# Opening of a two-layer hybrid trunk: first norm, modulation and first projection in an order fixed by hand

## The chip, the cores and the metric

One core of a Trainium2 chip runs the whole program. The metric is the time of one execution in device microseconds, taken over several runs; one further execution was recorded by the hardware profiler, and its trace is what the rows below come from. Engines are named as the profile names them: PE (TensorE, matmul), DVE (VectorE), ACT (ScalarE), POOL (GpSimd), SP (SyncE, which here only issues transfers).

## The reference, cut to what matters

The kernel computes two layers over 256 context tokens and 1024 latent tokens, 1280 in all, of width 1024. What the change touches is the first lines of the first layer:

```python
def rmsnorm(x):
    xf = x.astype(jnp.float32)
    return (xf * lax.rsqrt(jnp.mean(xf * xf, axis=-1, keepdims=True) + RMS_EPS)).astype(x.dtype)

def modulate(x, shift, scale):
    return rmsnorm(x) * (1.0 + scale) + shift

for layer in range(DEPTH):
    mod_l = (jax.nn.silu(c) @ w_ada[layer] + b_ada[layer])[:, None, :]
    mod_c = (jax.nn.silu(c_ctx) @ w_ada[layer] + b_ada[layer])[None, None, :]
    sh1_l, sc1_l, g1_l, sh2_l, sc2_l, g2_l = jnp.split(mod_l, 6, axis=-1)
    sh1_c, sc1_c, g1_c, sh2_c, sc2_c, g2_c = jnp.split(mod_c, 6, axis=-1)
    pl = split_proj(modulate(xl, sh1_l, sc1_l) @ w_in[layer])
    pc = split_proj(modulate(xc, sh1_c, sc1_c) @ w_in[layer])
    ...
```

Behind them come four chunkwise scans in both directions (the mixers), an output projection, a squared-ReLU MLP, and the same again for layer two.

## The kernel before

Activations lie feature-major: x is eight tiles of 128 features by 1280 tokens, and `k` counts these tiles. Tokens go in three blocks, `TBS`: 0 to 256 (context), 256 to 768 and 768 to 1280. Every float32 product is made of three matmuls, from a high part and a low part of each operand: `Hhi`, `Hlo` are the parts of the normalised input.

The opening has four pieces of work. First the modulation: `ada_unit` loads 32 pieces of `w_ada` (256 KB each, L382) on SP's queue into 16 slots and multiplies each by the silu of the two conditions (L383, four column groups of the array at a time); `ada_finish` copies, transposes and adds the bias (L389 to L400). Then the norm: `rstd` squares each tile on ACT (L447), adds the squares over features on PE (L448), spreads the sum (L451 ACT, L452 PE), and takes the logarithm and the exponential on ACT (L454, L455). Then `norm_apply`, tile by tile: DVE scales (L477), ACT adds the shift and rounds to `Hhi` (L480), DVE makes `Hlo` (L482). Last the first projection, `denseVS`: its weights `w_vs` (8 tiles, L590) are split on ACT and DVE (L591, L592), and for each of ten chunks of 128 tokens 24 matmuls of 128x304 run over k in one PSUM bank (L601), followed by two evacuations (L604, L605). Next in the program are the transposes of `turn` (L616), the dense products of the other heads (L294 to L296, weights split at L282 and L283), the features of the GLA heads (L787 on PE, L307 on ACT, L313 on DVE) and the scans.

Nothing here has a hand-fixed order: a scheduler sees the whole program and sets the order of every engine's instructions, so products and splits of different pieces interleave. That holds for the scans too: between two steps of a scan (L831, L956, L1000, L1019 on PE) it sets dense matmuls (L294 to L296, L632 to L634) and, on DVE, the next modulation rows (L414).

`params2` and `cond_rows`, some 35 small DVE operations and a store of the conditions to memory that POOL issues (L333), run early, while PE and DVE wait for `w_ada`.

Of the kernel before, what the change touches and what calls it, by code (L numbers as in the profile page):

```python
# [34 lines left out]
def R(ap):  # L35
    return ap.bitcast(F32R)


def F(ap):
    return ap.bitcast(F32)  # L40


class Ring:
# [154 lines left out]
class K:  # L198
# [176 lines left out]
        nc.scalar.activation(self.o["rtd"](24), lg, AF.Exp, scale=128.0)  # L375


    def ada_unit(self, l, r, k, bank, bufs):
        nc = self.nc
        for g in range(4):  # L380
            w = bufs.next()(512)
            nc.sync.dma_start(w, self.io["w_ada"][l, r, k, :, g, :])  # L382
            nc.tensor.matmul(self.bank(bank)[32 * g:32 * g + 32, :], lhsT=self.cc[:, k, :], rhs=w,  # L383
                             start=(k == 0), stop=(k == NK - 1), tile_position=(0, 32 * g))

    def ada_finish(self, l, r, bank, bank2, tmp):
        nc = self.nc
        s = tmp(512)
        nc.scalar.activation(s, self.bank(bank), AF.Copy)  # L389
        T = self.bank(bank2).rearrange("p (c q) -> p c q", q=128)  # L390
        for cb in range(4):
            nc.tensor.transpose(T[:, cb, :], s[:, cb * 128:(cb + 1) * 128], self.ident)
        Tv = self.bank(bank2).rearrange("p (c g j) -> p g c j", g=4, j=32)[:, :, :, 0:2]
        mo = self.mod[:, l, 16 * r:16 * r + 16, :].rearrange("p (g c) j -> p g c j", c=4)
        bb = self.bada[:, l, 16 * r:16 * r + 16].rearrange("p (g c) -> p g c", c=4)
        nc.vector.tensor_tensor(mo, Tv, bb.unsqueeze(3).to_broadcast([128, 4, 4, 2]), op=ALU.add)
        if r in (0, 2):
            a = 8 if r == 0 else 32
            m = self.mod[:, l, a:a + 8, :]
# [26 lines left out]
    def rstd(self, tb, fast=False):  # L426
# [31 lines left out]
    def norm_mod(self, l, tbs, sh, sc):  # L458

        rs = [self.rstd(tbs[0], FAST[0])]  # L460
        for i, tb in enumerate(tbs):
            if i + 1 < len(tbs):
                rs.append(self.rstd(tbs[i + 1], FAST[0]))
            self.norm_apply(l, tb, rs[i], sh, sc)
            yield
# [114 lines left out]
    def denseVS(self, S, sp):  # L580

        nc, t = self.nc, self.nc.tensor
        V = self.get(S, "V")(NC, 256)
        P = self.get(sp, "raw")(NC, 48)
        src = self.io["w_vs"][self.l]

        def load(k):
            raw = self.raw.next()(512)[:, 0:304]
            hi, lo = (R(self.wall.sub(608 * k + 304 * e, 304)(304)) for e in range(2))
            nc.sync.dma_start(raw, src[k])  # L590
            nc.scalar.activation(hi, raw, AF.Copy)  # L591
            nc.vector.tensor_tensor(lo, raw, F(hi), op=ALU.subtract)  # L592
            return hi, lo

        def body(w):
            for c in range(NC):
                ps = self.bank(self.dbanks.next())
                for k in range(NK):
                    h, u = self.hm(k, 128 * c, 128), w[k]
                    for i, (a, b) in enumerate(((0, 0), (0, 1), (1, 0))):  # L600
                        t.matmul(ps[:, 0:304], lhsT=h[a], rhs=u[b], start=(k + i == 0), stop=(k == NK - 1 and i == 2))  # L601
                    if k == 3:
                        yield 1500
                nc.scalar.activation(V[:, c, :], ps[:, 0:256], AF.Copy)  # L604
                nc.vector.tensor_copy(P[:, c, :], ps[:, 256:304])  # L605
                yield 1500
        return Dense(load, NK, body)

    def turn(self, sp):

# [777 lines left out]
    def mix_open(self, l):  # L1388

        self.otbs = TBS if l == 0 else TBS[1:]  # L1390
        pw, (self.wall,) = self.pool(f"pw{l}", [1024 * 5])
        self.wring = Ring([self.wall.sub(1024 * i, 1024) for i in range(5)])
        nx = NK * NT
        left = (self.rest - nx - 5 * 1024) // 8 * 8
        ph, hs = self.pool(f"ph{l}", [left])
        hp = self.heap = Heap(hs)
        self.dbanks = Ring((0, 1, 2))
        self.mb = Ring((4, 5, 6, 7))
        self.mpair = Ring((4, 6))
        self.obank = Ring((3,))  # L1400
        self.sp, self.gl = {}, {}
        vs = self.denseVS(self.gl, self.sp)
        vs.pre(NK)
# [6 lines left out]
        if l == 1:  # L1410
            self.norm_block(l, TBS[-1], 0, 8, fast=FAST[3])
        for (t0, n), _ in zip(TBS, blocks):
            for _ in range(n // 64):
                next(gen, None)
        next(gen, None)
# [157 lines left out]
def build(ctx, tc, io):  # L1573
    b = K(ctx, tc, io)
    b.setup()
    nc = b.nc
    b.l = 0
    b.openX()
    for k in range(NK):
        nc.scalar.dma_start(b.X[k][:, 0:CTX], io["xT"][:, k, 0:CTX])  # L1580
    b.params(b.tmps.next())

    ps, ss = b.pool("ps", [512] * 16)
    bk = b.banks.next()
    ring = Ring(ss)
    for k in range(NK):
        b.ada_unit(0, 0, k, bk, ring)
    b.ada_finish(0, 0, bk, b.banks.next(), b.tmps.next())
    ps.release()
    b.params2(b.tmps.next())  # L1590
    b.cond_rows(b.tmps.next())
    for l in range(2):
        b.l = l
        tbs = TBS if l == 0 else TBS[1:]
# [12 lines left out]
        aring = Ring(zip(cs[nw + nf::2], cs[nw + nf + 1::2]))  # L1607
# [4 lines left out]
        gen = ada1(cs[nw:nw + nf] + tmps.items[4:])  # L1612
# [68 lines left out]
def host(x, c, ctx, c_ctx, w_ada, b_ada, w_in, g_heads, hgrn_lb_logits, ml_gate_bias, rt_decay_logit,  # L1681
         gla_w_a, gla_b_a, w_out, w_ff1, w_ff2, g_final):
    A = {}
    ca = np.ascontiguousarray
# [23 lines left out]
    for d in range(2):  # L1708
        ga[:, 16 * d:16 * d + 16, d, :] = gla_w_a[:, d]
    A["gla_w"] = ga  # L1710
    A["w_ada"] = ca(w_ada[:1, :, :2048].reshape(1, 8, 128, 1, 4, 512).transpose(0, 3, 1, 2, 4, 5))
# [9 lines left out]
    vs = [seg(n) for n in ("gl_v", "gl_a_fwd", "gl_a_bwd")] + [iff[:, :, :, q, :].reshape(2, 1024, 8) for q in range(2)]  # L1721
# [20 lines left out]
```

## Time and profile before

| | us |
|---|---|
| median of 3 runs (lowest, highest) | 3277.83 (3273.87, 3279.31) |
| profiled execution | 3277.57 |
| its span in the trace | 3275.8 |
| PE busy in the span | 3188.0 |
| DVE busy in the span | 2098.3 |
| last matmul of the first projection ends | 90.15 from the span's start |

The profiled execution's time is that of the span and 1.8 us around it. Times in the rows are microseconds from the span's start.

### The profile page before, as it was taken

To read this page: it belongs to the slowest core of one execution; us is meant where nothing else is said; L and a number is where in the kernel's file an instruction comes from. 1 tells how busy PE (TensorE), PEld (TensorE's weight loads), DVE (VectorE), ACT (ScalarE), POOL (GpSimd) and SP (SyncE) were. 2 spreads that over 40 slices of the span, in tenths; PEclk is the share of its full clock that TensorE was granted. 3 is DMA by queue.
4 is the path that set the end of the run, shared out by engine and by line. 5 is a ranking of instruction groups with operands and counts; after the bars stand their busy time and mean duration, and the time that the engine had idled before them with its cause. 6 is when DMAs were issued, how large, how long until landed. Compare 5 with 4: busy or idle time off the path is not lost.

```text
span 3275.8 us, 52563 instructions
## 1 busy us (share of the span) xinstructions
PE 3188.0 (97%) x20681; PEld 2607.3 (80%) x20681; DVE 2098.3 (64%) x4333; ACT 1285.0 (39%) x2665; POOL 11.5 (0%) x42
## 2 busy tenths in 40 slices
PE   7999999999999999999999999999999999999998
PEld 4787788878888888888888677788778888888887
DVE  4778887776588845454545586876756555555546
ACT  4666564545332121212122575764444322222222
POOL 0000000000000000000000000000000000000000
PEclk9999899999999999999999999999999999999999
DMA  6115566345157511111111212333224111111111
GB/s 208 58 61 176 183 186 190 120 134 179 63 165 230 161 39 39 39 39 39 39 39 40 78 64 73 120 109 113 90 72 151 58 46 52 46 52 46 52 49 65
DMA packets 181953, 308.20 MB, mean 94 GB/s; under 512 B 21880, under 2 KB 51240, under 8 KB 181448
## 3 DMA queue, kind: packets, MB, share of 16 engines
q1 hardware_dynamic: 180376, 303.02, 28.8%
q8 instruction: 162, 2.65, 0.3%
q10 hardware_dynamic: 1296, 1.81, 0.2%
q14 instruction: 87, 0.71, 0.1%
q0 software_dynamic: 32, 0.01, 0.0%
HBM read 259.11 MB, written 45.65 MB: 93 GB/s over the span
## 4 chain that ended last, share of the span: by engine, by line
PE 81%; DVE 8%; DMA 6%; ACT 3%; issue 1%; SPq 0%; DVEq 0%; ACTq 0%
PE psum L294 22%; PE psum L295 21%; PE psum L296 21%; PE psum L831 2%; PE psum L601 2%; PE psum L834 1%; PE psum L818 1%; PE psum L632 1%; DMA ph<-w_adaR 1%; PE psum L634 1%; PE psum L633 1%; PE psum L1359 1%; PE psum L706 1%; PE psum L1019 1%; DMA ps<-w_ada 1%
## 5 line engine op out<-in xcount | busy, mean ns | idle before, releaser
L526 DVE SCALAR_TENSOR_TENSOR x<-psum,st,x 128x512 f32<-128x512 f32 (+1 forms) x648 | 440.7, 689 | 203.5 <-PE psum L296 202.8
L282 ACT ACTIVATE pc<-st 128x512 fp32r<-128x512 f32 x256 | 161.2, 632 | 854.4 <-PE psum L295 840.9
L295 PE MATMUL psum<-pc,pc 128*128 128x512 f32 (+1 forms) x1296 | 477.0, 368 | 6.0 <-DVE pc L506 6.0
L294 PE MATMUL psum<-pc,pc 128*128 128x512 f32 (+1 forms) x1296 | 476.1, 367 | 0.0
L296 PE MATMUL psum<-pc,pc 128*128 128x512 f32 (+1 forms) x1296 | 474.7, 366 | 0.0
L294 PE MATMUL psum<-Hhi,pc 128*128 128x512 f32 (+1 forms) x1280 | 471.1, 368 | 1.5 <-ACT pc L282 1.5
L295 PE MATMUL psum<-Hlo,pc 128*128 128x512 f32 (+1 forms) x1280 | 472.0, 369 | 0.1
L296 PE MATMUL psum<-Hhi,pc 128*128 128x512 f32 (+1 forms) x1280 | 470.5, 368 | 0.0
L294 PE MATMUL psum<-Hhi,pw 128*128 128x512 f32 (+1 forms) x1192 | 451.5, 379 | 7.6 <-ACT pw L282 3.5
L295 PE MATMUL psum<-Hlo,pw 128*128 128x512 f32 (+1 forms) x1192 | 447.5, 375 | 0.0
L296 PE MATMUL psum<-Hhi,pw 128*128 128x512 f32 (+1 forms) x1192 | 446.6, 375 | 0.6 <-DVE pw L283 0.6
L505 DVE TENSOR_TENSOR st<-st 128x256 f32<-128x256 f32 (+1 forms) x160 | 101.8, 637 | 301.5 <-ACT pc L504 300.8
L295 PEld LDWEIGHTS psum<-pc,pc 128*128 128x128 f32 x1296 | 245.0, 189 | 48.4 <-DVE pc L506 6.9
L294 PEld LDWEIGHTS psum<-pc,pc 128*128 128x128 f32 x1296 | 245.0, 189 | 44.1 <-DVE x L526 1.2
L296 PEld LDWEIGHTS psum<-pc,pc 128*128 128x128 f32 x1296 | 244.6, 189 | 42.9 <-issue 2.7
L294 PEld LDWEIGHTS psum<-Hhi,pc 128*128 128x128 f32 x1280 | 241.3, 189 | 43.3 <-ACT pc L282 2.4
L295 PEld LDWEIGHTS psum<-Hlo,pc 128*128 128x128 f32 x1280 | 241.3, 189 | 41.0 <-issue 0.5
L283 DVE TENSOR_TENSOR pc<-st,pc 128x512 fp32r<-128x512 f32 x256 | 175.6, 689 | 153.4 <-ACT pc L282 133.5
L296 PEld LDWEIGHTS psum<-Hhi,pc 128*128 128x128 f32 x1280 | 241.1, 188 | 41.0 <-DVE pc L283 0.6
L294 PEld LDWEIGHTS psum<-Hhi,pw 128*128 128x128 f32 x1192 | 227.3, 191 | 53.7 <-issue 9.2
L296 PEld LDWEIGHTS psum<-Hhi,pw 128*128 128x128 f32 x1192 | 227.1, 191 | 39.3 <-issue 2.4
L295 PEld LDWEIGHTS psum<-Hlo,pw 128*128 128x128 f32 x1192 | 227.6, 191 | 37.7 <-issue 2.9
(401 smaller groups left out, 4859.4 us busy)
## 6 DMA issues: line engine op xcount, KB each, us to landing
st<-w_ff SPq DMA_DIRECT2D x256, 256.0 KB
ph<-w_adaR SPq DMA_DIRECT2D x128, 256.0 KB
st<-w_inT SPq DMA_DIRECT2D x96, 256.0 KB
st<-w_adaR SPq DMA_DIRECT2D x74, 256.0 KB
pc<-w_adaR SPq DMA_DIRECT2D x54, 256.0 KB
st<-w_out SPq DMA_DIRECT2D x50, 256.0 KB
d_z<-st SPq DMA_DIRECT2D x40, 256.0 KB
ps<-w_ada SPq DMA_DIRECT2D x32, 256.0 KB
```

The costliest lines, as they stand in the source:

```text
L282: nc.scalar.activation(hi, raw, AF.Copy)
L283: (eng or nc.vector).tensor_tensor(lo, raw, F(hi), op=ALU.subtract)
L294: t.matmul(out, lhsT=w[0], rhs=m[0], start=first, stop=False)
L295: t.matmul(out, lhsT=w[0], rhs=m[1], start=False, stop=False)
L296: t.matmul(out, lhsT=w[1], rhs=m[0], start=False, stop=last)
L505: nc.vector.tensor_tensor(r, r, r, op=ALU.mult)
L526: nc.vector.scalar_tensor_tensor(x, ps, self.mod[:, l, 40 + o, j:j + 1], x, op0=ALU.mult, op1=ALU.add)
L601: t.matmul(ps[:, 0:304], lhsT=h[a], rhs=u[b], start=(k + i == 0), stop=(k == NK - 1 and i == 2))
L632: t.matmul(ps[:, e, :], lhsT=h[0], rhs=u[0], start=(k == 0), stop=False)
L633: t.matmul(ps[:, e, :], lhsT=h[0], rhs=u[1], start=False, stop=False)
L634: t.matmul(ps[:, e, :], lhsT=h[1], rhs=u[0], start=False, stop=(k == NK - 1))
L831: nc.tensor.matmul(o, lhsT=ST[r0:r0 + kd, c, d, :], rhs=qd[d](c)[r0:r0 + kd, :], start=(j == 0), stop=False, tile_position=(r0, 0))
```

## The change

All of the opening of layer 0 moves into one function, `open_first`, whose order holds as written (`manual_schedule`). Every load is on SP's queue. The first 768 tokens of x come first, in eight pieces of 384 KB; a two-element store that reads the fifth of them follows, and behind it come the weights. `w_ada` is laid out anew on the host, as four sets of eight pieces; set q holds what the tiles 2q and 2q+1 need, for shift and scale. The modulation of a set is 32 products of 128 columns (`products`, L402) instead of 8 of 512, so that 128 products replace 32 and the columns stay the same, then one transpose, two additions and one more (`shifts`, L411 to L418). The first two blocks of tokens go two tiles at a time: `apply` for a tile, then `part` for six chunks (c = 0 to 5, six PSUM banks at once), with the products of the next set between the two tiles' parts. The third block's squares, norm, `apply` and its four chunks come behind all of that, tile by tile. `params2` and `cond_rows` stand behind the opening now. Squares were added on PE before, too; the function that does it is written anew.

```diff
+    def open_first(self, vs):
+        aring = Ring([hp.alloc(512) for _ in range(10)])
...
+        def products(ws):
+            for k in range(NK):
+                for g in range(4):
+                    nc.tensor.matmul(self.bank(6)[32 * g:32 * g + 32, 0:128], lhsT=self.cc[:, k, :], rhs=ws[k][:, g, :],
+                                     start=(k == 0), stop=(k == NK - 1), tile_position=(0, 32 * g))
+            s = self.tmps.items[6](128)
+            nc.scalar.activation(s, self.bank(6)[:, 0:128], AF.Copy)
+            return s
...
+        sqs = Ring(self.tmps.items[5:8])
+        def squares(tb, bank):
+            t0, n = tb
+            acc = self.bank(bank)[:, 0:n]
+            for k in range(NK):
+                g = k % 4
+                sq = sqs.next()(n)
+                nc.scalar.activation(sq, self.X[k][:, t0:t0 + n], AF.Square)
+                nc.tensor.matmul(acc[32 * g:32 * g + 32, :], lhsT=self.ones32, rhs=sq, start=(k < 4), stop=(k >= 4),
+                                 tile_position=(0, 32 * g))
...
+        def apply(k, tbs):
+            todo = []
+            for tb in tbs:
...
+                nc.vector.scalar_tensor_tensor(t, self.X[k][:, t0:t0 + n], self.mod[:, 0, 8 + k, j:j + 1], rs[tb],
+                                               op0=ALU.mult, op1=ALU.mult)
+                nc.scalar.activation(R(hi), t, AF.Identity, bias=b)
+                todo.append((lo, t, b, hi))
+            for lo, t, b, hi in todo:
+                nc.vector.scalar_tensor_tensor(R(lo), t, b, hi, op0=ALU.add, op1=ALU.subtract)
+
+        one, two_ = TBS[:2], TBS[2]
+        with self.tc.manual_schedule():
+            self.params(self.tmps.items[3])
+            load_x(0, two)
+
+            nc.sync.dma_start(self.d_e[0, 0, 0:1, 0:2], self.X[4][0:1, 0:2])
+            ws = load_w(0)
+            vs.load_raw(0)
+            vs.load_raw(1)
+            s0 = squares(TBS[0], 0)
+            rms(TBS[0], 1, s0)
+            s1 = squares(TBS[1], 2)
+            s = products(ws)
+            rms(TBS[1], 3, s1)
+            shifts(0, s)
+            vs.split()
+            vs.split()
+            ws = load_w(1)
+            apply(0, one)
+            apply(1, one)
+            for q in range(4):
+                k = 2 * q
+                for c in range(6):
+                    vs.part(c, k, c)
+                if q < 3:
+                    vs.load_raw(k + 2)
+                    vs.load_raw(k + 3)
+                    s = products(ws)
+                    if q < 2:
+                        ws = load_w(q + 2)
+                    else:
+                        load_x(two, NT)
+                for c in range(6):
+                    if c == 3 and q < 3:
+                        shifts(q + 1, s)
+                        vs.split()
+                        vs.split()
+                    vs.part(c, k + 1, c)
+                if q < 3:
+                    apply(k + 2, one)
+                    apply(k + 3, one)
+            s = squares(two_, 6)
+            rms(two_, 7, s)
+            apply(0, (two_,))
+            apply(1, (two_,))
+            for c in range(6):
+                vs.evac(c, c)
+            last = (6, 0, 1, 7)
+            for k in range(NK):
+                if k + 2 < NK:
+                    apply(k + 2, (two_,))
+                for c in range(6, NC):
+                    vs.part(c, k, last[c - 6])
...
         if l == 0:
-            for t0, n in TBS[1:]:
-                for k in range(NK):
-                    self.nc.sync.dma_start(self.X[k][:, t0:t0 + n], self.io["xT"][:, k, t0:t0 + n])
-        gen = iter(vs)
-        blocks = self.norm_mod(l, TBS, 0, 8) if l == 0 else iter(TBS)
...
+            self.open_first(vs)
...
+        if l == 0:
+            self.params2(self.tmps.next())
+            self.cond_rows(self.tmps.next())
...
-    for k in range(NK):
-        b.ada_unit(0, 0, k, bk, ring)
```

Three places in the order show what moves. The first is SP, from the start of the program: the parameters and then `w_ada` stood at the head of its queue before (the pieces of x for the context were on ACT's queue).

```order
L250 DMA st_77<-params 128x416
L382 DMA ps_0_110<-w_ada 128x512
L382 DMA ps_1_111<-w_ada 128x512
L382 DMA ps_2_112<-w_ada 128x512
L382 DMA ps_3_113<-w_ada 128x512
```

Now it begins thus (`ph0_0_100` holds the ten slots of `w_ada`, `d_e_70` is the target of the small store):

```order
L389 DMA x0_4_89<-xT 128x768
L389 DMA x0_5_90<-xT 128x768
L389 DMA x0_6_91<-xT 128x768
L389 DMA x0_7_92<-xT 128x768
L466 DMA d_e_70<-x0_4_89 1x2
L395 DMA ph0_0_100<-w_ada 128x512 x8
L699 DMA st_77<-w_vs 128x304 x2
L395 DMA ph0_0_100<-w_ada 128x512 x8
```

The eight pieces of x and the store have moved ahead of the first weight piece, and each set of `w_ada` is followed by the two tiles of `w_vs` for the same pair.

The second place is DVE at the third block of tokens, the last of the first projection. Before, with the scaling at L477 and `Hlo` at L482 (`st_77` is a temporary, `Hhi_80` what ACT wrote; the first L482 here is still that of the second block's last tile):

```order
L477 SCALAR_TENSOR_TENSOR st_77<-x0_0_85,st_77 128x512
L482 SCALAR_TENSOR_TENSOR Hlo_81<-st_77,Hhi_80 128x512
L477 SCALAR_TENSOR_TENSOR st_77<-x0_1_86,st_77 128x512
L482 SCALAR_TENSOR_TENSOR Hlo_81<-st_77,Hhi_80 128x512
L605 COPY ph0_0_256<-psum_63 128x48 x2
L482 SCALAR_TENSOR_TENSOR Hlo_81<-st_77,Hhi_80 128x512
L477 SCALAR_TENSOR_TENSOR st_77<-x0_2_87,st_77 128x512
L605 COPY ph0_0_256<-psum_63 128x48
L477 SCALAR_TENSOR_TENSOR st_77<-x0_3_88,st_77 128x512
L482 SCALAR_TENSOR_TENSOR Hlo_81<-st_77,Hhi_80 128x512
```

Now, with the scaling at L454, `Hlo` at L459, a weight split at L283 and small operations of `params2` at L340 and behind:

```order
L454 SCALAR_TENSOR_TENSOR st_77<-x0_4_89,st_77 128x512
L459 SCALAR_TENSOR_TENSOR Hlo_81<-st_77,Hhi_80 128x512
L454 SCALAR_TENSOR_TENSOR st_77<-x0_5_90,st_77 128x512
L340 TENSOR_TENSOR st_77<-st_77 128x4
L283 TENSOR_TENSOR pw0_0_96<-st_77,pw0_0_96 128x512
L341 TENSOR_TENSOR st_77<-st_77 128x4
L342 TENSOR_TENSOR st_77<-st_77 128x4
L364 TENSOR_SCALAR st_77<-st_77 128x24
L459 SCALAR_TENSOR_TENSOR Hlo_81<-st_77,Hhi_80 128x512
L454 SCALAR_TENSOR_TENSOR st_77<-x0_6_91,st_77 128x512
```

Scaling and `Hlo` of one tile stand behind each other, so that the scaling of the next tile is queued behind an `Hlo` that waits for ACT; before, the scaling of x0_1 stood ahead of the `Hlo` of x0_0, and that of x0_3 ahead of the `Hlo` of x0_2.

The third place is PE in the last latent scan of layer 0, at the step that follows L831 (in the change L959 is L831, L962 is L834, L1147 is L1019 and L834 is L706). Before:

```order
L1000 MATMUL psum_63<-px0_0_693 64x64 x5
L632 MATMUL psum_63<-pw0_0_252,Hhi_80 128x256
L633 MATMUL psum_63<-pw0_0_252,Hhi_80 128x256
L634 MATMUL psum_63<-pw0_0_252,Hlo_81 128x256
L632 MATMUL psum_63<-pw0_0_252,Hhi_80 128x256
L633 MATMUL psum_63<-pw0_0_252,Hhi_80 128x256
L634 MATMUL psum_63<-pw0_0_252,Hlo_81 128x256
L831 MATMUL psum_63<-px0_0_693,ph0_0_256 128x128 x2
L632 MATMUL psum_63<-pw0_0_252,Hhi_80 128x256
```

Now:

```order
L959 MATMUL psum_63<-ph0_0_100 128x128 x2
L962 MATMUL psum_63<-px0_0_727 64x128 x2
L1147 MATMUL psum_63<-px0_0_727 32x2x32 x8
L1147 MATMUL psum_63<-ph0_0_100,st_77 32x2x32 x7
L834 MATMUL psum_63<-st_77 128x512
L1147 MATMUL psum_63<-ph0_0_100,st_77 32x2x32
L959 MATMUL psum_63<-px0_0_727,ph0_0_100 128x128 x2
L296 MATMUL psum_63<-Hhi_80,pw0_0_96 128x512
```

Dense matmuls that stood between scan rows here stand further behind now. Counted over the order: ahead of the first latent L956 there are 24 more 512-column matmuls of L294 to L296 than before and 24 more of 256 columns; ahead of the last one there are 57 fewer of 512 columns and 230 fewer of L632 to L634 (3 fewer of 256 columns of L294 to L296). On DVE, 51 of the 512-column rows of L414 stand between the first and the last latent L952, where 76 stood, and 15 of L283 where 20 stood. From the layer's output projection on, the two orders are the same.

## Rows read from the trace of the kernel before

**Rows 1.** The page, its span and busy time by engine.

```profile
span 3275.8 us, 52563 instructions
PE 3188.0 (97%) x20681; PEld 2607.3 (80%) x20681; DVE 2098.3 (64%) x4333; ACT 1285.0 (39%) x2665; POOL 11.5 (0%) x42
```

**Rows 2.** Busy time by stage: window, length, engines, PEclk, DMA share, GB/s.

```profile
10.00:20.00 10.00, 5.58 (x24) 1.27 (x24) 5.67 (x40) 3.64 (x15) 0.00 (x0) 1.00 0.99 302
20.00:30.00 10.00, 9.19 (x46) 2.58 (x47) 0.28 (x1) 2.72 (x7) 0.64 (x1) 1.00 1.01 369
```

**Rows 3.** The chain that ended last, 0 to 100: start, length, piece.

```profile
2.11 6.54 DMA ps<-w_ada
...
31.60 3.61 DMA x<-xT
...
37.03 0.48 DVE st L477
37.50 0.39 DVE pw L592
...
64.09 26.06 PE psum L601 x182
```

**Rows 4.** Timeline of PE in the opening: start, length, instruction, count.

```profile
14.42 4.52 PE L383 MATMUL psum<-ps,st 128*32 128x512 f32 x22
...
35.36 0.66 PE L392 MATMUL psum<-st 128*128 128x128 f32 x4 [0.69 <-ACT st L389]
...
38.24 0.41 PE L601 MATMUL psum<-pw,Hhi 128*128 128x304 f32 x1
38.62 1.04 PE L448 MATMUL psum<-st 128*32 128x512 f32 x2
...
42.61 0.83 PE L601 MATMUL psum<-pw,Hhi 128*128 128x304 f32 x4 [1.21 <-ACT Hhi L480]
```

**Rows 5.** Timeline of ACT in the opening.

```profile
24.83 1.54 ACT L447 ACTIVATE st<-x 128x256 f32<-128x256 f32 x4 [6.20 <-PE psum L448]
...
28.75 0.42 ACT L455 ACTIVATE st<-st 128x256 f32<-128x256 f32 x1
...
37.54 0.51 ACT L480 ACTIVATE Hhi<-st 128x256 fp32r<-128x256 f32 x1 [0.33 <-DVE st L477]
...
54.98 0.63 ACT L455 ACTIVATE st<-st 128x512 f32<-128x512 f32 x1
55.76 2.41 ACT L447 ACTIVATE st<-x 128x512 f32<-128x512 f32 x4
...
66.91 0.72 ACT L480 ACTIVATE Hhi<-st 128x512 fp32r<-128x512 f32 x1
```

**Rows 6.** Timeline of DVE at the end of the second block.

```profile
66.13 0.75 DVE L477 SCALAR_TENSOR_TENSOR st<-x,st 128x512 f32<-128x512 f32 x1
66.79 0.75 DVE L482 SCALAR_TENSOR_TENSOR Hlo<-st,Hhi 128x512 fp32r<-128x512 f32 x1
```

**Rows 7.** Timeline of PE in the mixers: dense and narrow matmuls.

```profile
134.88 1.14 PE L818 MATMUL psum<-ph,px 128*32 128x64 f32 x64
331.57 0.40 PE L295 MATMUL psum<-Hlo,pw 128*128 128x512 f32 x1
331.80 0.39 PE L296 MATMUL psum<-Hhi,pw 128*128 128x512 f32 x1
```

**Rows 8.** Busy time by stage in the mixers, columns as in rows 2.

```profile
300.00:345.00 45.00, 34.78 (x326) 26.69 (x325) 41.06 (x100) 27.31 (x56) 0.00 (x0) 0.86 0.40 126
334.00:560.00 226.00, 214.11 (x2031) 177.88 (x2032) 182.40 (x483) 124.19 (x279) 1.29 (x12) 0.96 0.58 184
335.00:353.00 18.00, 12.68 (x64) 8.77 (x63) 12.90 (x28) 8.03 (x16) 0.00 (x0) 0.53 0.27 88
```

**Rows 9.** Timeline of DVE: the first row of the GLA features.

```profile
92.78 0.48 DVE L313 TENSOR_SCALAR px<-psum,st 128x256 f32<-128x256 f32 x1 [0.15 <-ACT st L307]
```

**Rows 10.** DMA issues between 24 and 34: the store of `cond_rows`, size, us to landing.

```profile
d_c<-st POOLq DMA_DIRECT2D x1, 8.0 KB, 4.9
```

More of the change, by code (lines that the diff above doesn't have):

```diff
@@ L375, in params2 @@
         nc.scalar.activation(self.o["rtd"](24), lg, AF.Exp, scale=128.0)
[L378 to L399, printed above, removed]
-            nc.vector.tensor_scalar(m, m, 1.0, None, op0=ALU.add)
@@ new lines, in open_first, with load_x, load_w, shifts @@
+    def open_first(self, vs):
+        nc, io, hp = self.nc, self.io, self.heap
+        aring = Ring([hp.alloc(512) for _ in range(10)])
+        two = CTX + 512
+        rs = {}
+        tn = Ring(self.tmps.items[:4])
+        rbuf = [self.tR.items[0], self.tR.items[1], self.tR.items[0]]
+        def load_x(a, b):
+            for k in range(NK):
+                nc.sync.dma_start(self.X[k][:, a:b], io["xT"][:, k, a:b])
+        def load_w(q):
+            out = []
+            for k in range(NK):
+                w = aring.next()(4, 128)
+                nc.sync.dma_start(w, io["w_ada"][q, k])
+                out.append(w)
+            return out
+        def products(ws):
[6 more added lines that the diff above has]
+            return s
+        def shifts(q, s):
+            T = self.bank(7)[:, 0:128]
+            nc.tensor.transpose(T, s, self.ident)
+            T = T.rearrange("p (g j) -> p g j", j=32)
+            for e in range(2):
+                o = 8 * e + 2 * q
+                bb = self.bada[:, 0, o:o + 2].unsqueeze(2).to_broadcast([128, 2, 2])
+                nc.vector.tensor_tensor(self.mod[:, 0, o:o + 2, :], T[:, 2 * e:2 * e + 2, 0:2], bb, op=ALU.add)
+            m = self.mod[:, 0, 8 + 2 * q:10 + 2 * q, :]
+            nc.vector.tensor_scalar(m, m, 1.0, None, op0=ALU.add)
+        sqs = Ring(self.tmps.items[5:8])
+        def squares(tb, bank):
+            t0, n = tb
+            acc = self.bank(bank)[:, 0:n]
+            for k in range(NK):
+                g = k % 4
[3 more added lines that the diff above has]
+                                 tile_position=(0, 32 * g))
+            s = sqs.next()(n)
+            nc.scalar.activation(s, acc, AF.Copy)
+            return s
+        def rms(tb, bank, s):
+            t0, n = tb
+            bro = self.bank(bank)[:, 0:n]
+            nc.tensor.matmul(bro, lhsT=self.sel, rhs=s, start=True, stop=True)
+            r = rbuf.pop(0)(n)
+            nc.scalar.activation(r, bro, AF.Ln, bias=self.eps)
+            nc.scalar.activation(r, r, AF.Exp, scale=-0.5)
+            rs[tb] = r
+        def apply(k, tbs):
+            todo = []
+            for tb in tbs:
+                t0, n = tb
+                j = 0 if t0 < CTX else 1
+                t = tn.next()(n)
+                b = self.mod[:, 0, k, j:j + 1]
+                hi, lo = self.Hhi[:, k, t0:t0 + n], self.Hlo[:, k, t0:t0 + n]
+                nc.vector.scalar_tensor_tensor(t, self.X[k][:, t0:t0 + n], self.mod[:, 0, 8 + k, j:j + 1], rs[tb],
[51 more added lines that the diff above has]
+            last = (6, 0, 1, 7)
+            for k in range(NK):
+                if k + 2 < NK:
+                    apply(k + 2, (two_,))
+                for c in range(6, NC):
+                    vs.part(c, k, last[c - 6])
+            for c in range(6, NC):
+                vs.evac(c, last[c - 6])
+        hp.free(*aring.items)
+        self.banks = Ring(range(8))
@@ L1402, in mix_open @@
         vs = self.denseVS(self.gl, self.sp)
-        vs.pre(NK)
         if l == 0:
-            for t0, n in TBS[1:]:
-                for k in range(NK):
-                    self.nc.sync.dma_start(self.X[k][:, t0:t0 + n], self.io["xT"][:, k, t0:t0 + n])
-        gen = iter(vs)
-        blocks = self.norm_mod(l, TBS, 0, 8) if l == 0 else iter(TBS)
-        if l == 1:
+            self.open_first(vs)
+        else:
+            vs.pre(NK)
+            gen = iter(vs)
             self.norm_block(l, TBS[-1], 0, 8, fast=FAST[3])
[L1412 to L1415, printed above, removed]
+            for _ in gen:
+                pass
         self.poolX.release()
@@ L1578, in build @@
     b.openX()
-    for k in range(NK):
[L1580 to L1586, printed above, removed]
-        b.ada_unit(0, 0, k, bk, ring)
[L1588 to L1591, printed above, removed]
     for l in range(2):
@@ L1710, in host @@
     A["gla_w"] = ga
-    A["w_ada"] = ca(w_ada[:1, :, :2048].reshape(1, 8, 128, 1, 4, 512).transpose(0, 3, 1, 2, 4, 5))
+    A["w_ada"] = ca(w_ada[0, :, :2048].reshape(8, 128, 2, 4, 256).transpose(3, 0, 1, 2, 4).reshape(4, 8, 128, 4, 128))
     A["w_adaR"] = ca(w_ada.transpose(0, 2, 1).reshape(2, 3, 16, 128, 1024))
```

42 lines of the change are left out of this document (25 added, 17 removed).

## Prediction

> **What bounds the kernel now.** I read the page first: PE is busy for 3188.0 of 3275.8 us [rows 1], so a change of the opening can be worth only what PE stands idle there, or what later work it starts sooner. So the stages come next: 10 to 20 us PE is half idle while the queues move 302 GB/s, and 20 to 30 they move 369 [rows 2]. The chain of waits says the same: up to 31.6 it runs over pieces of `w_ada`, then over x (31.60), and from 64.09 over 182 matmuls of the first projection, 26.06 us long [rows 3]; 26.06/182 gives 0.143 a matmul, and 240 of them are 34.3 us. So x comes too late, since it is queued behind 8 MB of `w_ada`, and the projection starts at 38.24 and runs steadily only from 42.61 [rows 4]. Its last matmul ends at 90.15 (64.09 + 26.06).
>
> **The change, as a sum in us from the span's start.** It is made against the profiled execution, 3277.57, a quarter of a us under the median of 3277.83. What a measurement can tell from no change is about 0.2%, 6.5 us.
>
> A. *x first.* 3.15 MB of x and 0.97 MB of parameters and constants at 345 GB/s, my choice between 302 and 369 [rows 2], from 2.0 (the first piece began at 2.11 [rows 3]): landed at 13.9 (13.2 to 15.6).
>
> B. *Context norm.* The last square takes 0.4 (four take 1.54), and from the end of those squares (26.37) to the end of the exponential (28.75 + 0.42) it took 2.8 [rows 5]: 17.1.
>
> C. *Squares of the second block.* Eight at 2.41/4 = 0.60 on ACT [rows 5]: 21.9; the last addition on PE 1.04 [rows 4]: 23.0. PE has its queue in order, so the products wait behind.
>
> D. *Products of set 0.* The trace has no such matmul. L383's first 22, of 512 columns, took 0.205 each [rows 4]; if that is the lower clock, 128 columns at the upper one take 0.026, and 32 of them 0.8. If none overlap, L392's 0.66/4 = 0.165 [rows 4] gives 5.3. L818, 32 columns of the array wide too, has 1.14/64 = 0.018 for 64 columns [rows 7], 1.15 for 32 of 128. With a pass's start and end I take 1.8: 24.8.
>
> E. *Spread of the norm's sum, transpose, split, scale, round.* The spread 1.0 on PE (like the 512-column addition): 25.8. Then transpose 0.3, three small DVE operations 0.5, two splits at 0.39, scaling 0.48 [rows 3], rounding 0.51 [rows 5] and five handovers: first `part` at about 29, 9 us sooner than now.
>
> F. *Cycle of two tiles.* PE has 36 matmuls (5.15) and the products (1.8). Between products and next scaling lies the same chain, 0.3 + 0.5 + 0.8 + 0.48 + 0.51 = 2.6 and handovers; three chunks (1.29) cover it in part, so about 1.7 of PE stays empty: 8.7. Three cycles end at 55.2, the last pair (36 matmuls and a wait for its `Hlo`) at 61.0. Before, nothing of this was a cycle: splits and scalings of later tiles ran ahead.
>
> G. *Norm of the third block.* Three square buffers: three squares run ahead of PE, the other five wait for additions that stand behind the parts. Five at 0.60 from 61.0, with a buffer's return, end at 64.2, then addition 1.04, copy, logarithm and exponential at about 0.63 [rows 5], spread 1.0: 68.4. x's rest is long landed (2.1 MB and three weight sets, about 54).
>
> H. *Tail.* Here the order on DVE decides: scaling, then `Hlo` of the same tile, with ACT between. Before, L477 and L482 of different tiles follow each other at 0.66 [rows 6]. Now one tile costs scaling 0.75, rounding 0.72 [rows 5], `Hlo` to the next scaling 0.66 [rows 6] and two handovers: 2.19, where PE needs 12 x 0.143 = 1.72. Eight are 17.5: 85.9. The small operations of `params2` and four weight splits of 0.69 in between are partly under the rounding: 2.4 (0 to 5). The last ten matmuls: 1.4. Projection over at 89.7, against 90.15.
>
> I. *What PE did meanwhile.* Nine dense matmuls (0.233 each, 331.57 to 331.80 [rows 7]) and some transposes now stand in the tail's gaps: 2.6 of later work done.
>
> J. *Clock.* The idle time around 66 to 68 may cost a stretch at 1.2 GHz. After the wait at 335 the granted clock was 0.53 over 18 us with 12.68 of PE's work in it [rows 8], which cost up to 6. I take 1, since the tail leaves PE a fifth of its time free. The Trainium skill ("TensorE: Matmul & The Clock Gate", section "Why this matters for your kernels") advises against idle gaps between bursts of matmuls, after which the engine falls to its lower clock; the rows at 335 agree, and by that rule the cost would be nearer to the upper end.
>
> K. *Features.* `cond_rows` now stores behind the last `part`, the store lands 4.9 us after its issue [rows 10], and ACT's L307 of the GLA features waits for it: with a transpose and a copy ahead, L313 comes at about 96, not 92.78 [rows 9]. Dense matmuls lie beside it; uncovered it is 3. I take 0.
>
> L. *Mixers of layer 0.* The scheduler sets them anew. In the latent scans, 226 us now with PE 214.1 and DVE 182.4 busy [rows 8], the counts of the order take out 57 + 24 matmuls of 512 columns (18.9), 230 + 24 + 3 of 256 (about 30) and on DVE 25 rows of L414 and 5 splits (20): PE 165, DVE 162, the rest later. If scans end with PE, nothing is lost, and if they last as long as now, 48 us. Nearest is 300 to 345, where dense rows were as thin: DVE was busy for 41.06 of 45 [rows 8], 91%, and PE idle for 10.2. By it the scans take 162/0.91 = 178, PE idle for 13 of them against 12 now: +1, which I take. By the 81% of the whole stretch they take 200, idle 35: +23.
>
> Sum: (89.7 - 90.15) - 2.6 + 1 + 0 + 1 = -1.1, so 3276.5. The nine us at the start are spent in F, G and H.
>
> **Rivals.**
>
> *The gaps in the opening close* (faster). If splits and scalings run while PE does the last chunks, F loses its 1.7 three times, A gains 0.7 by the upper rate, and H loses its 2.4: -8.2, 3268. For it speaks that the three chunks cover half of the chain already; against it that DVE's queue is in order and its splits stand behind the transposed result. It decides if a pair takes 7.2 rather than 8.7.
>
> *Thin scans* (slower). Between two scan rows the dense matmuls are too few to cover DVE's and ACT's chain. With the scans at 85% of DVE (162/0.85 = 191, PE idle 26 against 12) they cost 14 instead of 1: 3289.5. For it: at 300 to 345 PE was idle for 10 of 45 us, with dense rows as thin [rows 8]. Against: two scans stand interleaved in the new order, so one may cover the other, and DVE has 20 us less to do. It decides once DVE's share in the latent scans falls under 88% (162/0.88 = 184: 7 us).
>
> *Half clock in the tail* (slightly slower). PE's idle time at 66 to 68 is followed by parts at half rate: 12 matmuls take 3.43 a tile instead of 2.19, for five tiles 6.2, and the first parts, after PE's wait for the norm at 26 to 29, lose 2.3 if they stay at half rate as long as L383's first 22 lasted [rows 4]. With 1 in the sum already that is +7.5: 3284. For it: the wait at 335 was followed by such a stretch [rows 8]. Against it: idle times up to 1.2 us in the opening [rows 4] left the granted clock at 1.00 in 20 to 30 [rows 2]. The Trainium skill's rule in J would bring this case about.
>
> *Weights not held* (no change). If the store goes out before x is there, `w_ada` shares the rate with x's last pieces: 2 MB at 345 is up to 6 on A at worst, 3 of which C hides, since squares follow x's pieces: 3279.5.
>
> **How the numbers follow.** Forecast 0.40, gaps close 0.28, thin scans 0.20, half clock 0.08, weights not held 0.04. The forecast's own range, from A (-0.7 to +1.7), D (-1 to +3.5 with four sets partly covered), H (-2.4 to +2.6) and K (to +3) taken together, is 3271 to 3283, within 0.2%. Faster by over 0.2%: 0.28, and a little of the forecast's lower edge, 0.30. Slower: 0.20, half of half clock and the upper edge of D and K, 0.26. Between: 0.44. The range leaves a tenth on either side: 3264, four under the faster rival, to 3291, a little over the slower one.
>
> **What the profile after would show.** Step A right: x's squares on ACT begin near 5 us and the last square of the second block ends near 22. E: first L717 at 29 rather than 38. F: PE idle between pairs about 1.7 us with DVE's scaling as releaser. H: L454 and L459 alternate with ACT's L456 between, 2.2 us a tile. J: PEclk of 0.5 somewhere in 66 to 75, or not. L: PE's idle time in the latent scans 13 us. The prediction is wrong if the last L717 ends before 84 or after 95, or if PE idles over 25 us in the latent scans.

## The result and the profile after

The changed kernel takes 3303.24 us (median of 4 runs, 3298.98 to 3306.64), the kernel before 3276.62 in the same session: a ratio of 1.008, 95% interval 1.0068 to 1.0093, so 22 to 30 us slower. The forecast was 3276.5 with a range to 3291. The profiled execution took 3298.98 and its span is 3297.2.

The page of the changed kernel, beside [rows 1]:

```profile
PE 3196.7 (97%) x20873; PEld 2621.5 (80%) x20873; DVE 2098.8 (64%) x4343; ACT 1288.6 (39%) x2668; POOL 11.5 (0%) x42
```

PE is busy 8.7 us more than before, though it does the same dense work, and idle 12.7 us more. Busy time that grows without work is the first sign of the lower clock. Two stages of the opening (columns as in [rows 2]):

```profile
30.00:40.00 10.00, 9.01 (x102) 8.18 (x102) 5.37 (x14) 3.43 (x7) 0.00 (x0) 0.85 0.63 202
70.00:80.00 10.00, 5.06 (x19) 4.60 (x20) 4.69 (x12) 5.47 (x12) 0.00 (x0) 0.70 0.01 2
```

The granted clock is 0.85 at 30 to 40 and 0.70 at 70 to 80, each time behind a wait of PE (3.51 us up to 28.78 and 2.98 us up to 72.78, both for ACT's `Hhi`). The chain of waits names what stands around the second one (start, length, piece):

```profile
62.96 1.03 PE psum L430 x6
...
64.65 3.35 PE psum L430 x10
...
68.67 1.14 PE psum L439 x2
...
71.21 0.76 DVE st L454
```

The third block's additions follow ACT's squares one by one (62.9 to 68.0), then copy, spread, logarithm, exponential, scaling and rounding run with nothing beside them on PE. The first `part` came at 28.8 (29 forecast) and the last one ended at 94.4 (89.7 forecast; 90.15 before). And what begins with that end begins later. SP's store of the mLSTM gate rows, and the ACT instruction on their last transfer, in the kernel before (timelines of SP and ACT):

```profile
92.42 0.67 SPq L1205 DMA_DIRECT2D d_if<-ph  x2
...
125.09 0.24 ACT L1260 ACTIVATE ph<-ph 128x40 f32<-128x40 f32 x1 [4.64 <-DMA ph<-d_a]
```

and in the changed one:

```profile
96.84 0.63 SPq L1333 DMA_DIRECT2D d_if<-ph  x2
...
130.12 0.24 ACT L1388 ACTIVATE ph<-ph 128x40 f32<-128x40 f32 x1 [1.98 <-DMA ph<-d_a]
```

33 us lie between in both; it is a chain of small transfers, and ACT's queue stands behind its end. In the changed kernel PE runs out of work there and waits for ACT, and the granted clock falls once more; in the kernel before PE has no such wait at this place. PE's timeline and the window behind the wait:

```profile
132.50 1.72 PE L946 MATMUL psum<-ph 128*32 128x64 f32 x56 [2.93 <-ACT ph L1022]
```

```profile
132.00:139.00 7.00, 6.50 (x75) 6.03 (x76) 3.42 (x8) 5.21 (x15) 0.00 (x0) 0.52 0.15 37
```

Last the latent scans, from the first latent L956 to the last: 334.1 to 555.4 before, 353.1 to 542.5 in the changed kernel (busy time by stage, before first):

```profile
334.10:555.40 221.30, 209.88 (x1999) 174.54 (x2000) 179.48 (x476) 120.72 (x270) 1.29 (x12) 0.96 0.58 182
```

```profile
353.10:542.50 189.40, 173.30 (x1659) 137.35 (x1659) 154.58 (x411) 109.26 (x244) 1.20 (x11) 0.86 0.48 154
```

The order has 48.7 us of dense work less there (18.9 + 29.9, step L). 209.9 - 48.7 is 161.2 of PE's work, and PE was busy for 173.3 at a granted clock of 0.86 instead of 0.96: by this estimate 12 us are the clock's. PE idles 16.1 us instead of 11.4. Together that is about 17 us; the two traced executions differ by 21.4, the medians by 27. The waits for which PE idles most there stand at L1147 (us in total, times, longest):

```profile
PE psum L1147 <- DVE px L1119: 5.9, 4, 2.6
```

### The profile page after: what moved, and what is told of

Its sections match the earlier page's. It is cut to its first block, busy times and chain, and to the rows that moved or that the text cites. A ratio compares the mean times of both kernels' runs of the same rounds, so it can differ in the third digit from the quotient of the medians.

```text
span 3297.2 us, 52938 instructions
## 1 busy us (share of the span) xinstructions
PE 3196.7 (97%) x20873; PEld 2621.5 (80%) x20873; DVE 2098.8 (64%) x4343; ACT 1288.6 (39%) x2668; POOL 11.5 (0%) x42
## 4 chain that ended last, share of the span: by engine, by line
PE 82%; DVE 10%; DMA 4%; ACT 3%; issue 1%; SPq 0%; DVEq 0%; ACTq 0%
PE psum L294 21%; PE psum L295 21%; PE psum L296 21%; PE psum L959 2%; PE psum L717 2%; PE psum L760 2%; PE psum L761 1%; PE psum L762 1%; PE psum L962 1%; PE psum L946 1%; PE psum L1147 1%; PE psum L834 1%; PE psum L1487 1%; DVE x L634 1%; PE psum L1084 1%
## 5 line engine op out<-in xcount | busy, mean ns | idle before, releaser
L634 DVE SCALAR_TENSOR_TENSOR x<-psum,st,x 128x512 f32<-128x512 f32 (+1 forms) x648 | 441.2, 690 | 204.0 <-PE psum L296 203.4
L282 ACT ACTIVATE pc<-st 128x512 fp32r<-128x512 f32 x256 | 161.2, 632 | 853.0 <-PE psum L295 828.3
L294 PE MATMUL psum<-pc,pc 128*128 128x512 f32 (+1 forms) x1296 | 476.5, 368 | 0.0
L296 PE MATMUL psum<-pc,pc 128*128 128x512 f32 (+1 forms) x1296 | 475.0, 367 | 0.0
L294 PE MATMUL psum<-Hhi,pc 128*128 128x512 f32 (+1 forms) x1280 | 471.1, 368 | 1.5 <-ACT pc L282 1.5
L296 PE MATMUL psum<-Hhi,pc 128*128 128x512 f32 (+1 forms) x1280 | 470.6, 368 | 0.3 <-DVE pc L283 0.3
L294 PE MATMUL psum<-Hhi,pw 128*128 128x512 f32 (+1 forms) x1192 | 457.0, 383 | 1.1 <-ACT st L816 0.7
L296 PE MATMUL psum<-Hhi,pw 128*128 128x512 f32 (+1 forms) x1192 | 448.4, 376 | 0.1
L294 PEld LDWEIGHTS psum<-pc,pc 128*128 128x128 f32 x1296 | 245.2, 189 | 44.1 <-DVE x L634 1.2
L296 PEld LDWEIGHTS psum<-pc,pc 128*128 128x128 f32 x1296 | 244.8, 189 | 42.9 <-issue 2.7
L294 PEld LDWEIGHTS psum<-Hhi,pc 128*128 128x128 f32 x1280 | 241.3, 189 | 43.2 <-ACT pc L282 2.4
L296 PEld LDWEIGHTS psum<-Hhi,pc 128*128 128x128 f32 x1280 | 241.2, 188 | 41.5 <-DVE pc L283 1.1
L283 DVE TENSOR_TENSOR pc<-st,pc 128x512 fp32r<-128x512 f32 x256 | 175.8, 690 | 154.4 <-ACT pc L282 134.7
L294 PEld LDWEIGHTS psum<-Hhi,pw 128*128 128x128 f32 x1192 | 229.3, 192 | 47.9 <-issue 10.0
L296 PEld LDWEIGHTS psum<-Hhi,pw 128*128 128x128 f32 x1192 | 228.9, 192 | 38.3 <-issue 2.1
```

The costliest lines, as they stand in the source:

```text
L283: (eng or nc.vector).tensor_tensor(lo, raw, F(hi), op=ALU.subtract)
L294: t.matmul(out, lhsT=w[0], rhs=m[0], start=first, stop=False)
L296: t.matmul(out, lhsT=w[1], rhs=m[0], start=False, stop=last)
L634: nc.vector.scalar_tensor_tensor(x, ps, self.mod[:, l, 40 + o, j:j + 1], x, op0=ALU.mult, op1=ALU.add)
```

## The experiments

What makes the scheduler set the scans of layer 0 otherwise? The ten slots of `w_ada` come from the heap, which hands out memory from a cursor on (next fit). They are given back, but the cursor stays 5,120 words further. Buffers that are taken later and no longer fit behind it then lie elsewhere, and the scheduler sets another order. Theory 1, **placement**: this is the loss, and the opening is nearly neutral. Theory 2, **the opening**: its longer tail, lower clock and late features cost the time, and the mixers only start later.

**The cursor set back** (the changed kernel; the scans' order is then that of the kernel before):

```diff
+        cur = hp.cur
         aring = Ring([hp.alloc(512) for _ in range(10)])
...
         hp.free(*aring.items)
+        hp.cur = cur
```

> The changed kernel with one thing undone: after the opening the heap's next-fit cursor is set back to where it stood before the ten slots of w_ada were taken, so that every buffer of the mixers lies where it lay before the change, and the order of the scans is again that of the kernel before (dense matmuls of 48 us of work are back between the scan steps). Theory 1 (placement: the ten slots move the heap's cursor, the scheduler then sets the scans of layer 0 with too few dense rows, and the opening itself is nearly neutral): between 3274 and 3282, that is within 0.2% of the kernel before, with 94 us still for the end of the first projection. Theory 2 (the opening itself costs the time: longer tail, lower clock, late GLA features, and the mixers lose because they start later): 3295 or more.

3285.74 us (8 runs; before 3276.63), ratio 1.0023 (1.0013 to 1.0034). Between the theories: two thirds of the loss are gone, and 8 us stay, which belong to the opening. In its latent scans everything is as before:

```profile
347.00:567.00 220.00, 209.73 (x1999) 174.54 (x2000) 179.48 (x476) 120.99 (x270) 1.28 (x12) 0.96 0.57 183
```

**The cursor moved in the kernel before**, nothing else:

```diff
         vs = self.denseVS(self.gl, self.sp)
+        if l == 0:
+            hp.free(*[hp.alloc(512) for _ in range(10)])
```

> The kernel before with one thing added: ten slots of 512 words are taken from the heap and given back at once, with nothing loaded into them, where the changed kernel takes its slots. The opening stays as it was; the order of the scans becomes that of the changed kernel. Theory 1 (placement): 3295 to 3305, some 20 to 25 us slower than before, with PE idle for about 18 us in the latent scans and the granted clock at half in stretches there. Theory 2 (the opening): 3277, no change.

3295.86 (6 runs), ratio 1.0062 (1.0048 to 1.0075). So placement alone costs 0.62%, the opening alone 0.23%, and both together 0.80%: they add up. The latent scans of this run, with the opening of before, look like those of the changed kernel:

```profile
345.30:532.80 187.50, 171.23 (x1659) 135.81 (x1659) 154.68 (x411) 108.80 (x244) 1.21 (x11) 0.89 0.48 155
```

**Six slots instead of ten**, a control: the cursor moves, the buffers still fit, the scans' order stays.

```diff
-            hp.free(*[hp.alloc(512) for _ in range(10)])
+            hp.free(*[hp.alloc(512) for _ in range(6)])
```

> The kernel before with six slots of 512 words taken from the heap and given back, instead of ten: the cursor moves, but the buffers that follow still fit behind it, and the order of the scans stays that of the kernel before. If it is the order of the scans that costs the time: 3275 to 3279, no change. If it is the addresses of the buffers that cost it: some of the 19 us that ten slots cost, 3285 or more.

3275.19 (10 runs; before 3276.14), ratio 0.9998 (0.9984 to 1.0011). A cursor that moves and leaves the order as it was costs nothing.

**One buffer placed elsewhere**, the cursor moved by ten: about half of the dense rows come back between the scan steps.

```diff
     def feat_v(self, vi, S):
+        if vi == 0 and self.l == 0:
+            S["V"] = self.heap.top(2560)
```

> The kernel before with the cursor moved by ten slots, as in the run that cost 19 us, and one buffer of the first hg pair (V, 2560 words) placed at the free end of its memory instead of at the next fit. The order of the scans then lies between the two: ahead of the last L956 stand 579 matmuls of L632 to L634 (710 before, 480 with the cursor moved) and 720 of 512 columns (729 and 672). If it is the dense rows missing between the scan steps that cost the time: a part of the 19 us is back, 3284 to 3290, with less PE idle and less time at the lower clock between the first latent L956 and the last. If it is another thing that the moved cursor brings (buffers that must be waited for): 3293 to 3298, as with the cursor moved alone.

3286.64 (10 runs; before 3275.51), ratio 1.0029 (1.0018 to 1.004): half of the loss is back for half of the rows. Its latent scans:

```profile
350.20:548.60 198.40, 183.53 (x1807) 151.47 (x1808) 165.84 (x439) 113.12 (x251) 1.37 (x12) 0.94 0.55 176
```

The granted clock is 0.96, 0.94, 0.89 and 0.86 in the kernel before, this one, the one with the cursor moved and the changed one; PE's idle time 11.4, 14.9, 16.3 and 16.1. Against the kernel before, and with the dense work that left counted off (25.7 us here, 48.7 with the cursor moved), the latent scans lose some 3 us here and 15 there. The other 8 us of this run are lost ahead of the first latent L956 (2.5 with the cursor moved alone), with PE idle for 6 of them. So the lower clock between the scan rows goes with the missing rows; what the moved buffer costs ahead of them stays open.

The next runs take the opening apart, all with the cursor set back.

**Scaling ahead in the tail.** On DVE the scaling of the next tile goes ahead of a tile's low part, and the six evacuations go ahead of the first low part.

```diff
-            apply(0, (two_,))
-            apply(1, (two_,))
+            todo = [scale(0, two_), scale(1, two_)]
             for c in range(6):
                 vs.evac(c, c)
+            low(*todo.pop(0))
...
                 if k + 2 < NK:
-                    apply(k + 2, (two_,))
+                    todo.append(scale(k + 2, two_))
+                if todo:
+                    low(*todo.pop(0))
```

> The kernel with the cursor set back, and in the third block's tail the scaling of a tile stands ahead of the low part of the tile before it on DVE, with the six evacuations ahead of the first low part. If the alternation on DVE and the evacuations behind it hold the tail (71.2 to 94.1 in the changed kernel), the first projection ends 2 to 4 us sooner and the whole is 2 to 4 us under the kernel with the cursor set back. If PE's lower clock at 74 holds it, the end moves by less than 1.

3281.08 (10 runs), ratio 1.0016 (1.0006 to 1.0026), 4.7 us under the one with the cursor set back; the first projection ended at 92.1, not 95.9. The order on DVE and the place of the evacuations, changed together here, were worth a little more than the 2 to 4 expected.

**The opening mended in three places**: as the last, the third block's squares ahead of the last six parts, `params2` and `cond_rows` at the head.

```diff
+        self.params(self.tmps.items[3])
+        self.params2(self.tmps.next())
+        self.cond_rows(self.tmps.next())
         with self.tc.manual_schedule():
-            self.params(self.tmps.items[3])
...
+                if q == 3:
+                    s = squares(two_, 6)
                 for c in range(6):
```

> As the one with the scaling ahead, and in addition the third block's squares stand ahead of the last six parts (k = 7), and the small operations of params2 and the store of cond_rows stand at the head of the program. If what the opening spends in its norm of the third block and its tail is really on the path, the first projection ends near 86 and the whole is 3268 to 3272; if later work is bound by DVE and ACT from there on, the sooner end is given back and it stays near 3277.

3284.68 (10 runs; one of them, 11543.54, is no part of the ratio), ratio 1.0028 (1.0017 to 1.0039): no gain. The small operations at the head hold PE's first addition of squares (10.95 instead of 8.76, with one of them on DVE, L358, as its releaser), the first `part` came at 32.2 instead of 30.4, and PE now stood behind squares (65.4 to 70.5) ahead of work that it could have done. The first projection ended at 94.7. A miss.

**Squares between the chunks**: one square's addition after each of eight of the twelve chunks of the last two tiles.

```diff
                     vs.part(c, k, c)
+                    if q == 3 and c > 0:
+                        square(c - 1)
...
+                    if q == 3 and c < 3:
+                        square(c + 5)
```

> Cursor set back, scaling ahead in the tail, and the third block's squares set between the chunks of the last two tiles' parts, with the norm's spread ahead of the last part. If PE's idle time around the norm of the third block (9 us of it between 62 and 75) is on the path: first projection over at about 87, 5 us sooner than with the scaling ahead alone, and the whole near 3276. If PE's work before the scans isn't what their start waits for, the whole stays at 3281.

3288.01 (6 runs; before 3276.14), ratio 1.0032 (1.0018 to 1.0046): worse, with the first projection over at 100.6. PE's timeline shows why:

```profile
62.34 1.92 PE L502 MATMUL psum<-st 128*32 128x512 f32 x2 [2.65 <-ACT st L500]
...
70.02 1.05 PE L502 MATMUL psum<-st 128*32 128x512 f32 x2
```

A single addition between other matmuls takes 1.05 us, and 1.92 at the lower clock that followed the wait; ACT's squares came late, behind the rounding of tile 7. Another miss.

**The store early**: the same, and `cond_rows` behind the parameters.

```diff
+            self.cond_rows(self.tmps.items[3], 4)
             load_x(0, two)
```

> As the one with the squares between, and the store of cond_rows stands behind the parameters at the head of the program, where PE and DVE are idle (params2 stays in the tail). If the late store holds the GLA features and these the scans (term K): the first L313 comes 3 us sooner after the end of the first projection, and the whole falls by 2 to 3. If the scans wait for the mLSTM gate rows' transfers, which start when the first projection ends and took 33 us to ACT's L1260 (92.4 to 125.1 before, 96.8 to 130.1 changed): no change against the one with the squares between.

3288.17 (7 runs), ratio 1.0039 (1.0026 to 1.0052), against 3288.01 without: no difference.

**PE kept busy, on the last one**: unused matmuls in two waits.

```diff
+        def idle(bank, n):
+            for _ in range(n):
+                nc.tensor.matmul(self.bank(bank)[0:32, :], lhsT=self.ones32, rhs=self.X[0][:, 0:512], start=True, stop=True)
...
             shifts(0, s)
+            idle(5, 5)
...
+            idle(6, 5)
```

> As the one with the early store, and PE does five matmuls that nothing uses in each of the two waits, behind the first transposes (26 to 29) and ahead of the third block's first parts, so that it stands idle less. If the lower clock at 30 to 34 and at 73 to 80 costs what it shows (3.4 and 6.8 us at half rate), and idle time is what brings it: those stretches go, and the end of the first projection comes 2 to 4 us sooner. If the waits' length alone decides, the end stays, or comes a microsecond later.

3283.39 (10 runs), ratio 1.0018 (1.0007 to 1.0029), some 5 us less. The first projection ended at 96.6, not 100.5, as expected.

**Kept busy, and nothing else**, on the kernel with the cursor set back (five and six matmuls):

> The kernel with the cursor set back and nothing else than eleven matmuls that nothing uses, five in PE's wait at 26 to 30 and six in its wait at 71 to 74. If the lower clock behind these waits (3.4 us at 31, 6.8 us at 75) is what the opening pays for them: both stretches go, the first projection ends 3 to 5 us sooner than the 95.9 of the kernel with the cursor set back, and the whole is 3280 to 3282. If the stretches come from elsewhere (the wait of 1.9 us at 75, PE half idle in the norm before), they stay and so does the time.

3281.69 (10 runs; before 3275.31), ratio 1.0018 (1.0007 to 1.0029), against 1.0023 without; the first projection ended at 92.8. The stretches at 31 and 75 are gone. The two intervals overlap, so the gain of the whole isn't settled by this run alone.

**Squares ahead**: into eight slots of `w_ada`, added in one batch behind the last parts; scaling ahead.

```diff
+                if q == 3:
+                    done = []
+                    for j in range(NK):
+                        done.append(aring.items[j](512))
+                        nc.scalar.activation(done[j], self.X[j][:, two:NT], AF.Square)
```

> Cursor set back, scaling ahead, and the third block's eight squares go into eight of the slots of w_ada, so that ACT makes them during the last two tiles' parts and PE adds them in one batch behind the parts. The norm of the third block then takes about 4 us less: first projection over at about 88 to 89, not 92.1. If the end of the first projection sets the rest (through the mLSTM gate rows' transfers, 34 us from that end to ACT's L1260): the whole is near 3277. If it doesn't: 3281, as with the scaling ahead alone.

3280.29 (10 runs), ratio 1.0014 (1.0004 to 1.0023), the first projection over at 90.0. The batch takes 2.83 us, where the additions of the changed kernel, one behind each square, took 5.1 (62.89 to 67.98):

```profile
64.18 2.83 PE L525 MATMUL psum<-ph,st 128*32 128x512 f32 x16
```

The end came a microsecond behind the forecast, the time stayed where it was: with an end like that of before, some 5 us are still lost. What the trace shows is the lower clock (windows 25 to 40 and 67 to 82):

```profile
25.00:40.00 15.00, 10.83 (x108) 8.97 (x106) 7.54 (x20) 5.96 (x13) 0.00 (x0) 0.89 0.71 238
67.00:82.00 15.00, 9.94 (x49) 8.43 (x49) 9.24 (x18) 9.38 (x19) 0.31 (x1) 0.77 0.00 1
```

**Squares ahead and kept busy**:

> As the one with the squares ahead, and eleven unused matmuls in the two waits, as in the run with these alone. If they keep the clock up: first projection over at 84 to 86, the whole 3270 to 3274, for the first time under the kernel before. If they don't: as the one with the squares ahead.

3272.73 (10 runs; before 3275.31), ratio 0.9991 (0.9982 to 1.0001): 7.6 us under the same without the unused matmuls, and as fast as the kernel before or a little faster. The first projection ended at 87.6 (84 to 86 expected). The same windows:

```profile
25.00:40.00 15.00, 14.02 (x128) 8.92 (x119) 8.31 (x21) 6.59 (x14) 0.00 (x0) 1.00 0.76 255
67.00:82.00 15.00, 15.00 (x76) 9.99 (x77) 11.14 (x21) 10.08 (x21) 0.00 (x0) 1.00 0.00 1
```

**All mended**: the last, and the store early.

> As the one before it, with the store of cond_rows at the head of the program. If the late store holds anything (term K): 1 to 3 us less than without. If the gate rows' transfers alone set the scans' start: the same time.

3274.47 (10 runs), ratio 0.9997 (0.9987 to 1.0006): the store early brings nothing.

## Why the prediction was wrong

The step that failed is L, the mixers of layer 0. It was put at +1, by the one stretch in which DVE was 91% busy, and cost about 20 us (1.0062 of 3276, 1.0048 to 1.0075) in the run with the cursor moved alone. The mechanism stood among the rivals as thin scans, at 0.20 and 14 us, and the count of the order was right: 48.7 us of dense work left the latent scans. The size failed because the step let a thin scan cost only what PE idles. DVE's share was 82% (154.58 of 189.40), not 91%, and the scans lasted 189.4 us, not 178. But PE idled for 16.1 us of them, near the 13 taken and far from the 26 of the rival and the 35 of the bound. The rest is PE's work, which the step priced at the upper clock and put at 165 (161 in the narrower window shown above): PE was busy for 173.3, and the lower clock took some 12 of the 17 us. Why the order changed was never asked in the prediction; it is the heap's cursor, shown both ways. Which buffer forces which dense row behind the scans stays open beyond the one that was moved.

The opening costs 8 us by itself (1.0013 to 1.0034), where the sum A to K gave -2.1. Point by point: A to E came out within a microsecond (last square of the context over at 13.9, first `part` at 28.8 against 29), though the first square began at 7.2 and not near 5; the products of sets 1 to 3 took 1.95 us each, with 1.8 taken. F was 10.2 in the first cycle, at the lower clock in part, and 9.0 in the two behind it, not 8.7: PE's gap was 1.0, not 1.7, but the parts with their transposition took 6.1, not 5.15. The last pair ended at 63.0, not 61.0. G took 8.2 against 7.4. H, the tail, took 23.2 from the third block's norm to the end, against 21.3: the term left out that two chunks wait for the evacuations of banks 0 and 1 behind the second low part (PE idle for 1.9 us with DVE's L722 as releaser), and the clock:

```profile
75.88 0.87 PE L717 MATMUL psum<-pw,Hhi 128*128 128x304 f32 x2 [1.92 <-DVE ph L722]
...
82.16 0.44 PE L717 MATMUL psum<-pw,Hhi 128*128 128x304 f32 x2
```

The same two matmuls take 0.87 at the lower level and 0.44 at the upper one. From 83 on the tail goes as H said. DVE's low parts start 2.2 us apart (82.82, 85.03, 87.35, 89.56, 91.81), each behind a wait for ACT or small operations in its place, and PE takes each up within 0.4 us of its end (timelines of DVE and PE):

```profile
85.03 0.75 DVE L459 SCALAR_TENSOR_TENSOR Hlo<-st,Hhi 128x512 fp32r<-128x512 f32 x1 [0.79 <-ACT Hhi L456]
...
86.01 0.30 PE L717 MATMUL psum<-pw,Hlo 128*128 128x304 f32 x1
```

PE's own part of a tile is 1.74 to 1.85 there, and dense matmuls of later work (I) fill the rest of the 2.2. The run with the scaling ahead bears this out: without the alternation the end came 3.8 us sooner.

I was booked as a gain of 2.6, and the traces show none left: dense work done early shortens what PE has to do beside the gate rows' 33 us of transfers, and these begin with the end of the first projection. In the changed kernel PE idles 2.9 us behind them, and the granted clock was 0.52 at 132 to 139. No run tests I by itself. The end of the first projection orders the runs with the cursor set back only roughly: 95.9, 92.1 and 87.6 gave 1.0023, 1.0016 and 0.9991, but 90.0 gave 1.0014 and 96.6 gave 1.0018. ACT's instruction behind the last transfer of the gate rows orders them better: it came at 137.7, 132.3, 131.4, 129.5, 126.8 and 123.4 (before: 125.1) where the ratio was 1.0032, 1.0023, 1.0018, 1.0016, 1.0014 and 0.9991. The other four lie off this row by no more than their intervals, farthest of them the opening mended in three places, at 130.2 with 1.0028 (1.0017 to 1.0039). Each time is of one traced execution, so this is an argument and not a test.

J was put at 1, with up to 6 as the bound. The half clock rival, at 0.08, had the right mechanism: matmuls without use in two waits brought 7.6 us in one pair of runs, whose intervals lie apart (1.0014 to 0.9991), and 4 to 5 in the other two. In that pair the stretch behind the gate rows' wait went too: the granted clock was 0.76 at 129 to 136 without the unused matmuls, and 1.00 at 125.6 to 132.6 with them. The 1.2 us of wait that the prediction set against this rival stands at 42.6, outside the window of 20 to 30 that it was read beside; the waits of the changed kernel were 3.5 and 3.0 us. The Trainium skill's advice against idle gaps between bursts ("TensorE: Matmul & The Clock Gate", "Why this matters for your kernels") agrees with the clock of 0.85 and 0.70 behind these two waits. K was right in the sum: the first L313 came at 98.0, not 96, but the store's place changed nothing, twice. That weights are held until x landed worked as written, and the clock rival's first stretch lay where it said, at 30.

The rival that the opening's gaps close did not come about: the cycles kept a gap of 1.0 us and took 9.0, not 7.2. The chances left 0.26 for slower, too little, since L's own bounds, +1 to +23, lay almost wholly on that side and were counted as a rival of 0.20.

## What to carry to other kernels

A change of one stage can move another through shared bookkeeping: an allocator's cursor, left elsewhere by buffers that are long given back, cost more than twice as much as the stage that was rewritten. Compare the order of the untouched stages first; if it differs, restore the state that stage starts from before judging the change.

Count PE's busy time against its work, not only its idle time: the scans with less filler paid by the clock as well. And before work done early is booked as a gain, look for a chain of transfers that starts at the end of the stage; whoever waits for it sees only the end of that chain.

## What the runs showed of the hardware

Unused matmuls in a wait made a kernel faster (3280.29 to 3272.73): with eleven of them in two waits of 3.5 and 3.0 us the granted clock was 1.00 at 25 to 40 and at 67 to 82, where it was 0.89 and 0.77 without. Eight 512-column additions in four column groups take 2.83 us as one batch, but 1.05 us each when other matmuls stand between them, which makes 8.4 for eight.
